# Weight-stationary blocks: three 256-column products into one set of PSUM columns, read in place, with PSUM dealt out anew

## Chip, cores and metric

One core of one Trainium2 chip. The metric is device time of one execution in microseconds. The core's engines that matter here are TensorE (PE for its matmuls, PEld for its weight loads), VectorE (DVE), ScalarE (ACT) and the DMA queue that SyncE (SP) issues. GpSimd does next to nothing.

## What is computed

Two layers of a decoder trunk on one sequence of 256 positions, D_MODEL 2048, all in fp32. Each layer projects the normed residual into many branches, mixes each branch (multi-scale pooling, latent attention "mla", short gated convolution, cross-attention into 256 memory rows), gates it with a SiLU path, projects it back, merges the four with sigmoid gates, and adds an output projection:

```python
h = rms_norm(x, norm_g[l])
proj = h @ w_in[l]
(pv, pz, cq, ckv, kr, mz, cb, cc, cx, cz, xq, xz, gpre) = jnp.split(proj, split_points, axis=-1)
y_pool = pool_mixer(pv, pool_w[l], pool_scale[l]) * silu(pz)
y_mla = mla_mixer(cq, ckv, kr, ...) * silu(mz)
y_conv = conv_mixer(cb, cc, cx, conv_w[l]) * silu(cz)
y_mem = memory_xattn(xq, mem_kv, ...) * silu(xz)
merged = sum(gates[:, :, i] * (y_i @ w_branch[l, i]) for the four branches)
x = x + merged @ w_out[l]
```

## The kernel before

Every large product is taken in split precision. A weight chunk of 128 x 1024 fp32 numbers is loaded (`raw`), ACT rounds it to fp32r (`hi`, line 304), and DVE takes the rest (`lo` = raw - hi, line 305). `raw` has 4 buffers, `hi` and `lo` 3 each. Activations are kept the same way in `op` tiles: for two 128-row halves, 256 columns of hi and then 256 columns of lo. A product is then hi*hi + hi*lo + lo*hi, added up in PSUM.

There are two kinds of blocks. In `tm_block` (lines 317 to 319) the activation is the stationary operand and 512 (288 or 384 in a few) columns of weights move: three matmuls for each piece of the sum. In `fm_block` the weight is stationary and the 256 positions move, which gives the result with channels on partitions. That is used for the branches mz, xz, pv, pz, cc, cx, cb and cz (four blocks of 256 channels each) and, through `fm_tile` alone, for the small `pool_w` products. One `fm_block` is 32 calls of `fm_tile` (two halves of 128 channels, 16 pieces of the sum); both layers have 64 such blocks and 8 small ones of 4 calls, 2080 calls in all. Each call is two matmuls:

```python
T.matmul(ps[:, j, :], hi[:, k, n0 : n0 + P], o[:, half].rearrange("p a s -> p (a s)"), start=first, stop=False)
T.matmul(ps[:, j, :S], lo[:, k, n0 : n0 + P], o[:, half, 0, :], start=False, stop=last)
```

The first multiplies weight hi with hi and lo of the activation side by side (512 columns of PSUM); the second adds weight lo times hi to the first 256. So a result sits in two sets of PSUM columns, and `fm_sum` adds them: ACT copies the second set to SBUF (`fmt`, line 337), DVE adds the first set to it (line 338).

PSUM has eight banks of 512 fp32 columns. The pool `acc` holds three tiles of two banks, which `tm_block` and `fm_block` take in turn; `ms` holds two tiles of one bank for transposes and attention. A block can start only when the readers of the tile whose place it takes are done.

The order of the work on each engine is made by a scheduler from the program order; weight loads and their `hi` and `lo` are put some way ahead. In the mla stage a written sequence of steps (`SEQUENCE`) mixes short `tm_block`s ("uq", "ukv"), attention steps and eight `fm_block`s (mz and xz). In the pool stage come four pv blocks, then twice: two pz blocks with SiLU (`silu_half`), and two small products with `pool_w`. The conv stage has sixteen blocks in a row.

Of the kernel before, what the change touches and what calls it, by code (L numbers as in the profile page):

```python
# [10 lines left out]
F32 = mybir.dt.float32  # L11
F32R = mybir.dt.float32r
I32 = mybir.dt.int32
AF = mybir.ActivationFunctionType
ALU = mybir.AluOpType
AX = mybir.AxisListType

P = 128
# [6 lines left out]
S = 256  # L25
# [85 lines left out]
def tile_hybrid_trunk(  # L111
# [3 lines left out]
    V, A, T = nc.vector, nc.scalar, nc.tensor  # L115
# [4 lines left out]
    op = ctx.enter_context(tc.tile_pool(name="op", bufs=16))  # L120
    tp = ctx.enter_context(tc.tile_pool(name="tp", bufs=7))
    sp = ctx.enter_context(tc.tile_pool(name="sp", bufs=4))
    accp = ctx.enter_context(tc.tile_pool(name="accp", bufs=3, space=bass.MemoryType.PSUM))
    msp = ctx.enter_context(tc.tile_pool(name="msp", bufs=2, space=bass.MemoryType.PSUM))

    uid = [0]
# [1 line left out]
    def nm(s):  # L128
        uid[0] += 1
        return f"{s}{uid[0]}"  # L130

    def t4(s):
        return tp.tile([P, 1152], F32, tag="t4", name=nm(s))

    def acc():
        return accp.tile([P, 2, 512], F32, tag="acc", name=nm("acc"))

    def ms():
        return msp.tile([P, 512], F32, tag="ms", name=nm("ms"))
# [4 lines left out]
    def t2(s):  # L144
        return tp.tile([P, 512], F32, tag="t2", name=nm(s), bufs=7)

    def opnd():
        return op.tile([P, 2, 2, S], F32R, tag="op", name=nm("op"))
# [29 lines left out]
    def gcol(vec, name, i):  # L178
        c = VEC_ROWS[name][0] + i
        return vec["gt"][:, c : c + 1]  # L180
# [112 lines left out]
    def wchunks(l, name, c0):  # L293
        off, n, nk, kt = plan[name, c0]
        m = nk * n
        for k0 in range(0, kt, nk):
            raw = wp.tile([P, 1024], F32, tag="raw", name=nm("raw"), bufs=4)
            hi = wp.tile([P, 1024], F32R, tag="hi", name=nm("hi"), bufs=3)
            lo = wp.tile([P, 1024], F32R, tag="lo", name=nm("lo"), bufs=3)
            o = off + P * n * k0  # L300
            step()
            with tc.high_priority(AHEAD):
                nc.sync.dma_start(raw[:, :m], weights[l, o : o + P * m].rearrange("(p m) -> p m", p=P))
                A.copy(hi[:, :m], raw[:, :m])  # L304
                V.tensor_tensor(lo[:, :m], raw[:, :m], hi[:, :m].bitcast(F32), ALU.subtract)  # L305
            yield k0, nk, kt, n, *(w[:, :m].rearrange("p (k n) -> p k n", n=n) for w in (hi, lo))
# [13 lines left out]
        return ps  # L320

    def fm_tile(ps, j, hi, lo, o, half, k, n0, first, last):
        T.matmul(ps[:, j, :], hi[:, k, n0 : n0 + P], o[:, half].rearrange("p a s -> p (a s)"), start=first, stop=False)  # L323
        T.matmul(ps[:, j, :S], lo[:, k, n0 : n0 + P], o[:, half, 0, :], start=False, stop=last)  # L324

    def fm_block(rhs, l, name, c0):
        ps = acc()
        for k0, nk, kt, n, hi, lo in wchunks(l, name, c0):
            for j in range(2):
                for k in range(nk):  # L330
                    kk = k0 + k
                    fm_tile(ps, j, hi, lo, rhs[kk // 2], kk % 2, k, j * P, kk == 0, kk == kt - 1)
        return ps

    def fm_sum(dst, ps):
        tmp = t2("fmt").rearrange("p (n s) -> p n s", n=2)
        A.copy(tmp, ps[:, :, S:])  # L337
        V.tensor_tensor(dst, ps[:, :, :S], tmp, ALU.add)  # L338

    def split(o, src):  # L340
        A.copy(o[:, :, 0, :], src)
        V.tensor_tensor(o[:, :, 1, :], src, o[:, :, 0, :].bitcast(F32), ALU.subtract)
# [145 lines left out]
    def silu_half(z, i, h, l, c0):  # L488
        ps = fm_block(h, l, "in", c0 + 256 * i)
        sl = slice(2 * i, 2 * i + 2)  # L490
        fm_sum(z[:, sl, :], ps)
        sg = t2("sg").rearrange("p (n s) -> p n s", n=2)
        A.activation(sg, z[:, sl, :], AF.Sigmoid)  # L493
        V.tensor_tensor(z[:, sl, :], z[:, sl, :], sg, ALU.mult)  # L494

    def silu_tile():
        return t4("z")[:, :1024].rearrange("p (n s) -> p n s", n=4)
# [1 line left out]
    def silu_block(h, l, c0):  # L499
        z = silu_tile()  # L500
        for i in range(2):
            silu_half(z, i, h, l, c0)
        return z
# [226 lines left out]
    def pool_branch(l, vec, h):  # L730
        mixed = []
        for b in range(2):
            for i in range(2):
                ps = fm_block(h, l, "in", OFF["pv"] + 512 * b + 256 * i)
                g = 2 * b + i
                w = WINDOWS[g]
                v = t4("pv")[:, :544].rearrange("p (n s) -> p n s", n=2)
                nc.gpsimd.memset(v[:, :, :16], 0.0)
                fm_sum(v[:, :, 16:], ps)
                s = v  # L740
                sh = 1
                while sh < w:
                    n = t4("ps")[:, :544].rearrange("p (n s) -> p n s", n=2)
                    a = 2 * sh - 1
                    V.tensor_tensor(n[:, :, a:], s[:, :, a:], s[:, :, a - sh : 272 - sh], ALU.add)
                    s = n
                    sh *= 2
                fix = cst[:, C_FIX + 16 * g : C_FIX + 16 * (g + 1)].unsqueeze(1).broadcast_to([P, 2, 16])
                V.tensor_tensor(s[:, :, 16:32], s[:, :, 16:32], fix, ALU.mult)
                V.scalar_tensor_tensor(s[:, :, 16:], s[:, :, 16:], 1.0 / w, v[:, :, 16:], ALU.mult, ALU.subtract)  # L750
                o = opnd()
                split(o, s[:, :, 16:])
                mixed.append(o)
        ys = []
        for b in range(2):
            sz = silu_block(h, l, OFF["pz"] + 512 * b)
            (_, _, _, _, hi, lo), = wchunks(l, "pool", 512 * b)
            for i in range(2):
                g = 2 * b + i
                ps = acc()  # L760
                for j in range(2):
                    for k in range(2):
                        fm_tile(ps, j, hi, lo, mixed[g], k, 2 * i + k, j * P, k == 0, k == 1)
                y = t2("yp").rearrange("p (n s) -> p n s", n=2)
                fm_sum(y, ps)
                for j in range(2):
                    V.scalar_tensor_tensor(
                        y[:, j, :], y[:, j, :], gcol(vec, "pool_scale", 2 * g + j), sz[:, 2 * i + j, :], ALU.mult, ALU.mult
                    )
                o = opnd()  # L770
                split(o, y)
                ys.append(o)
        return ys

    def conv_branch(l, vec, h):
        ys = []
        for b in range(2):
            cc = t4("cc")[:, :1024].rearrange("p (n s) -> p n s", n=4)
            for i in range(2):
                ps = fm_block(h, l, "in", OFF["cc"] + 512 * b + 256 * i)  # L780
                fm_sum(cc[:, 2 * i : 2 * i + 2, :], ps)
            u = t4("u")[:, :1032].rearrange("p (n s) -> p n s", n=4)
            nc.gpsimd.memset(u[:, :, :2], 0.0)
            for i in range(2):
                ps = fm_block(h, l, "in", OFF["cx"] + 512 * b + 256 * i)
                sl = slice(2 * i, 2 * i + 2)
                fm_sum(u[:, sl, 2:], ps)
                V.tensor_tensor(u[:, sl, 2:], u[:, sl, 2:], cc[:, sl, :], ALU.mult)
            y = cc
            for n in range(4):  # L790
                w = [gcol(vec, "conv_w", 8 * j + 4 * b + n) for j in range(3)]
                V.tensor_scalar(y[:, n, :], u[:, n, 0:S], w[0], None, ALU.mult)
                V.scalar_tensor_tensor(y[:, n, :], u[:, n, 1 : S + 1], w[1], y[:, n, :], ALU.mult, ALU.add)
                V.scalar_tensor_tensor(y[:, n, :], u[:, n, 2 : S + 2], w[2], y[:, n, :], ALU.mult, ALU.add)
            bb = t4("cb")[:, :1024].rearrange("p (n s) -> p n s", n=4)
            for i in range(2):
                ps = fm_block(h, l, "in", OFF["cb"] + 512 * b + 256 * i)
                sl = slice(2 * i, 2 * i + 2)
                fm_sum(bb[:, sl, :], ps)
                V.tensor_tensor(y[:, sl, :], y[:, sl, :], bb[:, sl, :], ALU.mult)  # L800
            sz = silu_block(h, l, OFF["cz"] + 512 * b)
            ys += gated_out([y], [sz])
        return ys
# [58 lines left out]
    for l in range(DEPTH):  # L862
# [4 lines left out]
        vec = vecs[l]  # L867
# [28 lines left out]
        def filler(_):  # L896
            dst, name, b, i = fill.pop(0)
            if i == 0:
                dst[b] = silu_tile()
            silu_half(dst[b], i, h, l, OFF[name] + 512 * b)  # L900
# [7 lines left out]
        o, sz = xq, sxz  # L908
# [75 lines left out]
```

## Time and profile before

| | |
|---|---|
| median of 3 runs | 2520.2 us (2517.4 to 2521.82) |
| span of the profiled execution | 2517.2 us, so 3.0 us less than the median of the runs |
| PE busy | 2503.9 us, 99% of the span |
| DVE busy, ACT busy | 1539.0 us (61%), 1248.4 us (50%) |
| DMA | 484 MB, mean 192 GB/s |
| TensorE clock granted | full speed in all 40 slices |

Which of the three runs the profile belongs to is not recorded. The time of a PE matmul in the profile runs from its start to a modelled end, and neighbours overlap; what a matmul costs a dense stream is the distance from its start to the next one's start. A timeline row gives the start in microseconds, then the duration, engine, line, operation, the tiles, the shape and a count.

### The profile page before, as it was taken

The numbers are of one execution on the slowest core, as the hardware profiler recorded it, in microseconds if no ns is written. First come the engines' busy times: TensorE is split into PE (matmuls) and PEld (weight loads), VectorE is DVE, ScalarE is ACT, GpSimd is POOL, SyncE is SP. The second block draws the span as 40 slices with busy tenths as digits, with TensorE's granted clock in tenths as the row PEclk, the third lists the DMA queues.
The fourth block names the chain that finished last, engine by engine and source line by source line (L and its number), as shares of the span: only waits on it lengthen the run. The fifth ranks groups of instructions, "written<-read, shape, count | busy, mean of one in ns | idle before, by whom it ended". The sixth has DMA issues, their size and how long they took to land.

```text
span 2517.2 us, 32451 instructions
## 1 busy us (share of the span) xinstructions
PE 2503.9 (99%) x12402; PEld 2108.3 (84%) x12402; DVE 1539.0 (61%) x2132; ACT 1248.4 (50%) x1707; POOL 1.6 (0%) x16
## 2 busy tenths in 40 slices
PE   8999999999999999999999999999999999999999
PEld 7888888888888888888888888888888888888887
DVE  6767775566556655556474577755765565555554
ACT  7556674445444444445454566744444444444443
POOL 0000000000000000000000000000000000000000
PEclk9999999999999999999999999999999999999999
DMA  8665436655655566667655654366556655566565
GB/s 314 207 198 162 145 128 197 202 188 192 201 196 186 188 221 203 201 195 231 220 187 167 202 166 136 128 202 204 186 191 202 194 187 188 193 202 203 189 229 164
DMA packets 143676, 484.22 MB, mean 192 GB/s; under 512 B 16160, under 2 KB 17184, under 8 KB 143520
## 3 DMA queue, kind: packets, MB, share of 16 engines
q1 hardware_dynamic: 142800, 481.06, 58.5%
q8 instruction: 97, 1.59, 0.3%
q10 hardware_dynamic: 720, 1.09, 0.1%
q14 instruction: 59, 0.48, 0.1%
HBM read 477.89 MB, written 4.19 MB: 192 GB/s over the span
## 4 chain that ended last, share of the span: by engine, by line
PE 97%; DVE 1%; ACT 1%; DMA 0%; issue 0%; DVEq 0%; SPq 0%; ACTq 0%
PE acc L319 22%; PE acc L318 22%; PE acc L317 22%; PE acc L323 19%; PE acc L324 10%; PE ms L703 1%; PE ms L702 1%; PE ms L350 1%; DVE lo L305 0%; ACT junk L197 0%; PE ms L551 0%; PE ms L552 0%; PE ms L553 0%; DMA row<-in_x_dram 0%; ACT hi L304 0%; PE ms L722 0%
## 5 line engine op out<-in xcount | busy, mean ns | idle before, releaser
L305 DVE TENSOR_TENSOR lo<-raw,hi 128x1024 fp32r<-128x1024 f32 (+2 forms) x884 | 1062.4, 1202 | 869.8 <-ACT hi L304 867.0
L304 ACT CAST hi<-raw 128x1024 fp32r<-128x1024 f32 (+2 forms) x884 | 914.7, 1035 | 1179.1 <-PE acc L319 791.2
L317 PE MATMUL acc<-hi,op 128*128 128x512 f32 (+2 forms) x2496 | 962.5, 386 | 5.8 <-ACT op L392 5.7
L318 PE MATMUL acc<-lo,op 128*128 128x512 f32 (+2 forms) x2496 | 957.9, 384 | 1.7 <-DVE lo L305 1.7
L319 PE MATMUL acc<-hi,op 128*128 128x512 f32 (+2 forms) x2496 | 958.1, 384 | 0.0
L323 PE MATMUL acc<-op,hi 128*128 128x512 f32 x2080 | 736.9, 398 | 0.1
L324 PE MATMUL acc<-op,lo 128*128 128x256 f32 x2080 | 585.7, 282 | 0.0
L317 PEld LDWEIGHTS acc<-hi,op 128*128 128x128 f32 x2496 | 469.2, 188 | 95.2 <-ACT op L392 6.2
L319 PEld LDWEIGHTS acc<-hi,op 128*128 128x128 f32 x2496 | 469.0, 188 | 92.0 <-issue 1.3
L318 PEld LDWEIGHTS acc<-lo,op 128*128 128x128 f32 x2496 | 469.4, 188 | 91.1 <-DVE lo L305 2.9
L323 PEld LDWEIGHTS acc<-op,hi 128*128 128x128 f32 x2080 | 390.8, 188 | 94.3 <-DVE z L338 0.8
L324 PEld LDWEIGHTS acc<-op,lo 128*128 128x128 f32 x2080 | 392.9, 189 | 1.9 <-issue 1.3
L814 DVE TENSOR_TENSOR g<-acc,gb 128x1024 f32<-128x1024 f32 x32 | 39.2, 1224 | 12.7 <-PE acc L319 12.7
L337 ACT COPY fmt<-acc 128x512 f32<-128x512 f32 x72 | 41.4, 581 | 0.0
L815 ACT ACTIVATE g<-g 128x1024 f32<-128x1024 f32 x32 | 34.0, 1062 | 6.7 <-DVE g L814 6.7
L821 DVE TENSOR_TENSOR g<-g,acc 128x1024 f32<-128x1024 f32 x24 | 29.3, 1221 | 9.8 <-PE acc L319 9.8
L822 DVE TENSOR_TENSOR merged<-merged,g 128x1024 f32<-128x1024 f32 x24 | 29.2, 1219 | 0.0
L513 ACT ACTIVATE sm<-sm,smx,rqs 128x128 f32<-128x128 f32 (+1 forms) x32 | 17.3, 540 | 22.3 <-DVE smx L511 22.3
L494 DVE TENSOR_TENSOR z<-z,sg 128x512 f32<-128x512 f32 x32 | 22.0, 688 | 7.8 <-ACT sg L493 7.7
L197 ACT ACTIVATE junk<-acc 128x256 f32<-128x256 f32 (+2 forms) x68 | 25.2, 371 | 2.1 <-PE acc L319 1.2
L392 ACT ACTIVATE op<-ms,gt 128x256 fp32r<-128x256 f32 x32 | 15.1, 471 | 14.0 <-DVE op L393 14.0
L338 DVE TENSOR_TENSOR z<-acc,fmt 128x512 f32<-128x512 f32 x32 | 21.9, 684 | 0.0
(193 smaller groups left out, 949.1 us busy)
## 6 DMA issues: line engine op xcount, KB each, us to landing
raw<-in_weights_dram SPq DMA_DIRECT2D x836, 512.0 KB, 3.5
raw<-in_weights_dram SPq DMA_DIRECT2D x32, 288.0 KB, 2.8
gb<-in_gate_b_dram SPq DMA_DIRECT2D x32, 256.0 KB, 4.4
raw<-in_weights_dram SPq DMA_DIRECT2D x16, 384.0 KB, 3.1
mt<-in_memT_dram SPq DMA_DIRECT2D x14, 256.0 KB, 5.7
row<-in_mem_dram SPq DMA_DIRECT2D x4, 512.0 KB, 8.4
row<-in_x_dram SPq DMA_DIRECT2D x4, 512.0 KB, 8.2
xt<-in_xT_dram SPq DMA_DIRECT2D x8, 256.0 KB, 5.5
```

The source lines that it names most:

```text
L304: A.copy(hi[:, :m], raw[:, :m])
L305: V.tensor_tensor(lo[:, :m], raw[:, :m], hi[:, :m].bitcast(F32), ALU.subtract)
L317: T.matmul(ps[:, t, :n], hh, hi[:, k, :], start=kk == 0, stop=False)
L318: T.matmul(ps[:, t, :n], hh, lo[:, k, :], start=False, stop=False)
L319: T.matmul(ps[:, t, :n], hl, hi[:, k, :], start=False, stop=kk == kt - 1)
L323: T.matmul(ps[:, j, :], hi[:, k, n0 : n0 + P], o[:, half].rearrange("p a s -> p (a s)"), start=first, stop=False)
L324: T.matmul(ps[:, j, :S], lo[:, k, n0 : n0 + P], o[:, half, 0, :], start=False, stop=last)
L337: A.copy(tmp, ps[:, :, S:])
L814: V.tensor_tensor(g, pg, gb.unsqueeze(1).broadcast_to([P, 2, 512]), ALU.add)
L815: A.activation(g, g, AF.Sigmoid)
L821: V.tensor_tensor(g, g, pb, ALU.mult)
L822: V.tensor_tensor(mg, mg, g, ALU.add)
```

## The change

`fm_tile` now issues three matmuls of 256 columns, all into the same 256 PSUM columns: weight hi times activation hi, weight hi times activation lo, weight lo times activation hi. Both 128-channel halves of a block fit one bank, in a new tile `fm` (two buffers in the pool of `ms`); the bank is cleared once, by the first matmul of the first half. `acc` goes from three tiles to two and is left to `tm_block`. PSUM is full before (3 x 2 + 2 banks) and after (2 x 2 + 2 + 2). The sum on DVE is gone: `silu_half`, the pool products and the conv stage read the PSUM tile where they need it, twice in `silu_half` (the sigmoid on ACT, the product on DVE); pv and cc are copied out by ACT. The number of 128-row columns that TensorE streams is the same (512 + 256 = 3 x 256); the matmuls grow by 2080.

```diff
--- before.py
+++ after.py
@@ -120,7 +120,7 @@
     op = ctx.enter_context(tc.tile_pool(name="op", bufs=16))
     tp = ctx.enter_context(tc.tile_pool(name="tp", bufs=7))
     sp = ctx.enter_context(tc.tile_pool(name="sp", bufs=4))
-    accp = ctx.enter_context(tc.tile_pool(name="accp", bufs=3, space=bass.MemoryType.PSUM))
+    accp = ctx.enter_context(tc.tile_pool(name="accp", bufs=2, space=bass.MemoryType.PSUM))
     msp = ctx.enter_context(tc.tile_pool(name="msp", bufs=2, space=bass.MemoryType.PSUM))
 
     uid = [0]
@@ -134,6 +134,9 @@
 
     def acc():
         return accp.tile([P, 2, 512], F32, tag="acc", name=nm("acc"))
+
+    def fms():
+        return msp.tile([P, 2, S], F32, tag="fm", name=nm("fm"))
 
     def ms():
         return msp.tile([P, 512], F32, tag="ms", name=nm("ms"))
@@ -320,11 +323,13 @@
         return ps
 
     def fm_tile(ps, j, hi, lo, o, half, k, n0, first, last):
-        T.matmul(ps[:, j, :], hi[:, k, n0 : n0 + P], o[:, half].rearrange("p a s -> p (a s)"), start=first, stop=False)
-        T.matmul(ps[:, j, :S], lo[:, k, n0 : n0 + P], o[:, half, 0, :], start=False, stop=last)
+        wh, wl = hi[:, k, n0 : n0 + P], lo[:, k, n0 : n0 + P]
+        T.matmul(ps[:, j, :], wh, o[:, half, 0, :], start=first and j == 0, stop=False, skip_group_check=True)
+        T.matmul(ps[:, j, :], wh, o[:, half, 1, :], start=False, stop=False, skip_group_check=True)
+        T.matmul(ps[:, j, :], wl, o[:, half, 0, :], start=False, stop=last, skip_group_check=True)
 
     def fm_block(rhs, l, name, c0):
-        ps = acc()
+        ps = fms()
         for k0, nk, kt, n, hi, lo in wchunks(l, name, c0):
             for j in range(2):
                 for k in range(nk):
@@ -333,9 +338,7 @@
         return ps
 
     def fm_sum(dst, ps):
-        tmp = t2("fmt").rearrange("p (n s) -> p n s", n=2)
-        A.copy(tmp, ps[:, :, S:])
-        V.tensor_tensor(dst, ps[:, :, :S], tmp, ALU.add)
+        A.copy(dst, ps)
 
     def split(o, src):
         A.copy(o[:, :, 0, :], src)
@@ -488,10 +491,9 @@
     def silu_half(z, i, h, l, c0):
         ps = fm_block(h, l, "in", c0 + 256 * i)
         sl = slice(2 * i, 2 * i + 2)
-        fm_sum(z[:, sl, :], ps)
         sg = t2("sg").rearrange("p (n s) -> p n s", n=2)
-        A.activation(sg, z[:, sl, :], AF.Sigmoid)
-        V.tensor_tensor(z[:, sl, :], z[:, sl, :], sg, ALU.mult)
+        A.activation(sg, ps, AF.Sigmoid)
+        V.tensor_tensor(z[:, sl, :], ps, sg, ALU.mult)
 
     def silu_tile():
         return t4("z")[:, :1024].rearrange("p (n s) -> p n s", n=4)
@@ -757,15 +759,14 @@
             (_, _, _, _, hi, lo), = wchunks(l, "pool", 512 * b)
             for i in range(2):
                 g = 2 * b + i
-                ps = acc()
+                ps = fms()
                 for j in range(2):
                     for k in range(2):
                         fm_tile(ps, j, hi, lo, mixed[g], k, 2 * i + k, j * P, k == 0, k == 1)
                 y = t2("yp").rearrange("p (n s) -> p n s", n=2)
-                fm_sum(y, ps)
                 for j in range(2):
                     V.scalar_tensor_tensor(
-                        y[:, j, :], y[:, j, :], gcol(vec, "pool_scale", 2 * g + j), sz[:, 2 * i + j, :], ALU.mult, ALU.mult
+                        y[:, j, :], ps[:, j, :], gcol(vec, "pool_scale", 2 * g + j), sz[:, 2 * i + j, :], ALU.mult, ALU.mult
                     )
                 o = opnd()
                 split(o, y)
@@ -784,20 +785,17 @@
             for i in range(2):
                 ps = fm_block(h, l, "in", OFF["cx"] + 512 * b + 256 * i)
                 sl = slice(2 * i, 2 * i + 2)
-                fm_sum(u[:, sl, 2:], ps)
-                V.tensor_tensor(u[:, sl, 2:], u[:, sl, 2:], cc[:, sl, :], ALU.mult)
+                V.tensor_tensor(u[:, sl, 2:], ps, cc[:, sl, :], ALU.mult)
             y = cc
             for n in range(4):
                 w = [gcol(vec, "conv_w", 8 * j + 4 * b + n) for j in range(3)]
                 V.tensor_scalar(y[:, n, :], u[:, n, 0:S], w[0], None, ALU.mult)
                 V.scalar_tensor_tensor(y[:, n, :], u[:, n, 1 : S + 1], w[1], y[:, n, :], ALU.mult, ALU.add)
                 V.scalar_tensor_tensor(y[:, n, :], u[:, n, 2 : S + 2], w[2], y[:, n, :], ALU.mult, ALU.add)
-            bb = t4("cb")[:, :1024].rearrange("p (n s) -> p n s", n=4)
             for i in range(2):
                 ps = fm_block(h, l, "in", OFF["cb"] + 512 * b + 256 * i)
                 sl = slice(2 * i, 2 * i + 2)
-                fm_sum(bb[:, sl, :], ps)
-                V.tensor_tensor(y[:, sl, :], y[:, sl, :], bb[:, sl, :], ALU.mult)
+                V.tensor_tensor(y[:, sl, :], y[:, sl, :], ps, ALU.mult)
             sz = silu_block(h, l, OFF["cz"] + 512 * b)
             ys += gated_out([y], [sz])
         return ys
```

The scheduler moves little else. Three places bear on the prediction. The first is DVE in the pool stage of the first layer, around the end of the second pz block and the two small products; there, `z` is the SiLU tile, `yp` the pool result, `lo` a weight chunk, `gt` the small vectors. Before:

```order
L305 TENSOR_TENSOR lo_5339<-raw_5337,hi_5338 128x1024
L305 TENSOR_TENSOR lo_5361<-raw_5359,hi_5360 128x1024
L338 TENSOR_TENSOR z_5102<-acc_5198,fmt_5287 128x512
L305 TENSOR_TENSOR lo_5383<-raw_5381,hi_5382 128x1024
L494 TENSOR_TENSOR z_5102<-z_5102,sg_5290 128x512
L338 TENSOR_TENSOR yp_5308<-acc_5299,fmt_5309 128x512
L338 TENSOR_TENSOR yp_5326<-acc_5317,fmt_5327 128x512
L767 SCALAR_TENSOR_TENSOR yp_5308<-yp_5308,gt_83,z_5102 128x256
```

Now, on the same engine at the same place:

```order
L308 TENSOR_TENSOR lo_5751<-raw_5749,hi_5750 128x1024
L308 TENSOR_TENSOR lo_5781<-raw_5779,hi_5780 128x1024
L496 TENSOR_TENSOR z_5454<-fm_5579,sg_5700 128x512
L768 SCALAR_TENSOR_TENSOR yp_5722<-fm_5709,gt_83,z_5454 128x256 x2
L345 TENSOR_TENSOR op_5725<-yp_5722,op_5725 128x2x256
L768 SCALAR_TENSOR_TENSOR yp_5741<-fm_5728,gt_83,z_5454 128x256
```

The second pz block is `acc_5198` before and `fm_5579` now. Its last reader was the sum of line 338, behind `lo_5361`; now it is the product of line 496, behind `lo_5781`, the same two chunks further on. The two small products were `acc_5299` and `acc_5317` and are `fm_5709` and `fm_5728`.

The second place is PE at the same point: the last call of `fm_tile` of the first small product and the first of the second. Now:

```order
L327 MATMUL fm_5709<-op_5046,hi_5704 128x256
L328 MATMUL fm_5709<-op_5046,hi_5704 128x256
L329 MATMUL fm_5709<-op_5046,lo_5705 128x256
L327 MATMUL fm_5728<-op_5179,hi_5704 128x256
L328 MATMUL fm_5728<-op_5179,hi_5704 128x256
```

With two `fm` tiles in turn, `fm_5728` takes the place of `fm_5579`; before, the third `acc` tile stood between, and it was the next pz block that took the place of `acc_5198`.

The third place is PE in the mla stage, where the block "uq" of the first head pair (`acc_1943`) ends and its "ukv" (`acc_1994`) begins. Before:

```order
L318 MATMUL acc_1943<-lo_1964,op_1358 128x384
L319 MATMUL acc_1943<-hi_1963,op_1358 128x384
L317 MATMUL acc_1994<-hi_1996,op_1678 128x512
L318 MATMUL acc_1994<-lo_1997,op_1678 128x512
L319 MATMUL acc_1994<-hi_1996,op_1678 128x512
```

Now:

```order
L321 MATMUL acc_1943<-lo_1964,op_1358 128x384
L322 MATMUL acc_1943<-hi_1963,op_1358 128x384
L530 MATMUL ms_2079<-cst,qr_1913 128x128 x4
L530 MATMUL ms_2104<-cst,qr_1913 128x128
L320 MATMUL acc_1994<-hi_1996,op_1678 128x512
```

Five transposes of `qr` that stood behind `acc_1994` now stand in front of it. `acc_1994` now takes the place of the second "xq" block (`acc_1754`), two `tm_block`s back.

## Prediction

> **What bounds the kernel now.** I read the page's busy times first, then the chain that ended last, then the waits of PE.
>
> ```profile
> span 2517.2 us, 32451 instructions
> PE 2503.9 (99%) x12402; PEld 2108.3 (84%) x12402; DVE 1539.0 (61%) x2132; ACT 1248.4 (50%) x1707; POOL 1.6 (0%) x16
> PEclk9999999999999999999999999999999999999999
> PE 97%; DVE 1%; ACT 1%; DMA 0%; issue 0%; DVEq 0%; SPq 0%; ACTq 0%
> PE acc L319 22%; PE acc L318 22%; PE acc L317 22%; PE acc L323 19%; PE acc L324 10%; PE ms L703 1%; PE ms L702 1%; PE ms L350 1%; DVE lo L305 0%; ACT junk L197 0%; PE ms L551 0%; PE ms L552 0%; PE ms L553 0%; DMA row<-in_x_dram 0%; ACT hi L304 0%; PE ms L722 0%
> L323 PE MATMUL acc<-op,hi 128*128 128x512 f32 x2080 | 736.9, 398 | 0.1
> L324 PE MATMUL acc<-op,lo 128*128 128x256 f32 x2080 | 585.7, 282 | 0.0
> L337 ACT COPY fmt<-acc 128x512 f32<-128x512 f32 x72 | 41.4, 581 | 0.0
> L338 DVE TENSOR_TENSOR z<-acc,fmt 128x512 f32<-128x512 f32 x32 | 21.9, 684 | 0.0
> L814 DVE TENSOR_TENSOR g<-acc,gb 128x1024 f32<-128x1024 f32 x32 | 39.2, 1224 | 12.7 <-PE acc L319 12.7
> ```
>
> ```profile
> PE acc L317 <- ACT op L392: 5.7, 1, 5.7
> PE acc L318 <- DVE lo L305: 1.7, 1, 1.7
> PE ms L680 <- DVE yf L725: 0.5, 2, 0.2
> ```
>
> PE is the bound: 97% of the chain, at the full clock throughout. All that the view of waits shows of PE standing idle is 7.9 us, nearly all of it for work of the start (lines 392 and 305). So the 72 copies and 72 sums that vanish (41.4 us of ACT, some 49 us of DVE at 0.684) buy nothing directly: no PE time waits on them. What counts is how fast PE streams the 2080 tiles of lines 323 and 324, 29% of the chain, and whether new waits for PSUM appear.
>
> **The pace of the stream.** The durations of matmul rows overlap, so I take start to start. First and last rows of long stretches, from timelines of PE:
>
> ```profile
> 859.99 0.40 PE L323 MATMUL acc<-op,hi 128*128 128x512 f32 x1
> 876.59 0.40 PE L323 MATMUL acc<-op,hi 128*128 128x512 f32 x1
> ...
> 228.16 0.39 PE L323 MATMUL acc<-op,hi 128*128 128x512 f32 x1
> 231.97 0.39 PE L323 MATMUL acc<-op,hi 128*128 128x512 f32 x1
> ...
> 340.22 0.28 PE L552 MATMUL ms<-op,op 128*128 128x256 f32 x1
> 340.33 0.28 PE L553 MATMUL ms<-op,op 128*128 128x256 f32 x1
> 340.45 0.28 PE L551 MATMUL ms<-op,op 128*128 128x256 f32 x1
> ...
> 342.85 0.28 PE L324 MATMUL acc<-op,lo 128*128 128x256 f32 x1
> ...
> 929.83 0.39 PE L317 MATMUL acc<-hi,op 128*128 128x512 f32 x1
> 940.71 0.39 PE L317 MATMUL acc<-hi,op 128*128 128x512 f32 x1
> ...
> 122.46 0.30 PE L317 MATMUL acc<-hi,op 128*128 128x288 f32 x1
> 123.92 0.30 PE L319 MATMUL acc<-hi,op 128*128 128x288 f32 x1
> ```
>
> - Today's tile, 512 + 256 columns: 47 tiles in 16.60 us in the conv stage, 353 ns each. A count over the stage agrees:
>
> ```profile
> 727.00:895.00 168.00, 168.00 (x477) 89.40 (x476) 1.00 0.56 187
> ```
>
>   That is line 323 alone: 168.00 us over 476 loads is 353 ns. In parts of the mla stage the same tile takes 346 ns (11 tiles in 3.81 us). Why there are two paces the profile does not tell.
> - 512 columns alone (`tm_block`): 48 matmuls in 10.88 us, 227 ns.
> - 288 columns alone: 11 in 1.46 us, 133 ns. From these two, (227 - 133) / 224 = 0.42 ns a column and some 12 ns for each matmul whatever its size; 256 columns should then take 119 to 120 ns.
> - 256 columns alone, in cross-attention: 21 matmuls from 340.33 to 342.85, 2.52 us, 120 ns; the first two gaps are shorter, 0.23 us together. This is the nearest row: lines 551 to 553 are hi*hi, hi*lo, lo*hi of 256 columns, each with its own weight load, three in a row into one set of PSUM columns, which is what the new `fm_tile` does.
>
> **The change part by part.**
>
> 1. Three matmuls for two. Columns are equal, the fixed part is paid once more. A new tile is 3 x 120 = 360 ns against 353: +7 ns, 2080 x 6.7 = +13.9 us. Of the 512 tiles of the mla stage I count half as running at 346 ns today; for those 256 it is 7 ns more, +1.8 us. The ends: 115 ns, the first two gaps of that stretch, would give 345 and -16 us; 133 ns, the longest sustained row, would give 399 and +97 us. I take 120, since that row has size, loads and target of the new work; the short gaps do not last, and 133 belongs to 288 columns and holds only if a short burst flatters the 120.
>
> The Trainium skill, "TensorE: Matmul & The Clock Gate", section Back-to-back issue gap, gives N / 2.4 + 2.5 ns for a warm matmul. By it the tile would go from 216 + 109 = 325 to 3 x 109 = 328 ns, an estimate of +5 us over all tiles; the trace has 227 where it says 216 and 120 where it says 109, so the fixed part here is some 12 ns and not 2.5, and the measurement decides.
>
> 2. The second weight load of the same weights. `tm_block` already issues two matmuls in a row with one stationary operand (lines 317 and 318) and loads it twice; the page counts as many loads as matmuls (12402 each). I cost the extra 2080 loads at nothing beyond the 120 ns, since the 120 rows carry one load each. If the stream did not cover them, the 133 ns of the 288-column rows would be the nearest upper bound (the +97 us of step 1).
>
> 3. Two `fm` tiles where three `acc` tiles served: the pool stage. The timelines of PE, DVE and ACT around the end of the second pz block:
>
> ```profile
> 567.36 0.40 PE L323 MATMUL acc<-op,hi 128*128 128x512 f32 x1
> ...
> 568.77 0.40 PE L323 MATMUL acc<-op,hi 128*128 128x512 f32 x1
> ...
> 570.06 0.28 PE L324 MATMUL acc<-op,lo 128*128 128x256 f32 x1
> 570.40 0.49 PE L323 MATMUL acc<-op,hi 128*128 128x512 f32 x1
> ```
>
> ```profile
> 567.44 1.05 ACT L304 CAST hi<-raw 128x1024 fp32r<-128x1024 f32 x1 [1.73 <-PE acc L323]
> ...
> 568.52 1.23 DVE L305 TENSOR_TENSOR lo<-raw,hi 128x1024 fp32r<-128x1024 f32 x1 [1.55 <-ACT hi L304]
> 569.66 0.68 DVE L338 TENSOR_TENSOR z<-acc,fmt 128x512 f32<-128x512 f32 x1
> ```
>
> ```profile
>   PEld acc L317: 0.8, 2
>   PEld acc L323: 0.8, 2
> ```
>
> The pz block ends at 567.36. Its chunk frees a weight buffer, ACT and DVE convert the next chunk first, and the last reader of the pz tile ends only at 569.66 + 0.68 = 570.34. The next pz block, third in the ring, starts at 570.40, 0.06 later, though the stream was due at 570.18: a wait of 0.22 us, one of four that line 338 causes (last fence). In the new order the product of line 496 stands behind the same conversion, so it ends near 570.35 (0.69 long). But now the second small product needs that place, and the first is done at 567.36 + 4 x 0.36 = 568.80. PE waits 570.41 - 568.80 = 1.6 us, less the 0.22 of today: +1.4 us, four times, +5.6 us. Behind it nothing is late: the next pz block needs line 768 on the first small product, two instructions of 0.48 (today's line 767), done at 571.3, and PE gets there at 571.85. If the reader were served before the conversion, the wait would shrink to about nothing; if one more conversion slips ahead, it grows by 1.2 each.
>
> ```profile
> L767 DVE SCALAR_TENSOR_TENSOR yp<-yp,gt,z 128x256 f32<-128x256 f32 x16 | 7.0, 478 | 0.0
> ```
>
> 4. Two `acc` tiles for `tm_block`. The tight place is "ukv" of the first pair:
>
> ```profile
> 198.06 0.39 PE L317 MATMUL acc<-hi,op 128*128 128x512 f32 x1
> ...
> 198.60 0.19 ACT L197 ACTIVATION_READ_ACCUMULATOR junk<-acc 128x1 f32 x1
> ...
> 225.39 0.60 PE L680 MATMUL ms<-cst,qg 128*128 128x128 f32 x4
> 225.83 0.60 PE L685 MATMUL ms<-cst,kn 128*128 128x128 f32 x4
> ```
>
> It started at 198.06 and would now have to wait for the last sum of squares of "xq", 198.79. Five transposes moved in front fill 5 x 0.11 = 0.55 us of that; some 0.2 us is left, in each layer: +0.4 us. In the gate stage DVE reads a block as soon as it is done and needs 1.2 us (line 814), and the block behind it takes eight or sixteen pieces of six matmuls of 227 ns, 11 us or more; nothing waits there.
>
> 5. Removed work on ACT and DVE: cost nothing, gain nothing, since PE covers them; if PE were to speed up, DVE at 61% would still have room.
>
> Sum: 13.9 + 1.8 + 5.6 + 0.4 = +21.7 us, from a span of 2517.2 to 2538.9; with the 3.0 us between span and median, 2542 us.
>
> **Rivals.**
>
> A. The 256s do not hold 120 ns in a long stream. For it: the 120 is seen over some 23 matmuls only, and today's mixed tile runs at 353 though 227 + 120 makes 347, so a slip of 6 to 7 ns a tile exists. Against it: 512s and 288s alone hold their pace. With the same slip, 367 ns, a further 14 us on the forecast: 2556 us. It decides from 121 ns a matmul up.
>
> The same page of the Trainium skill, section Wait — 56ns, not 53.3ns?, says that a matmul decoded by firmware costs 62 ns of the sequencer; were a load to cost as much, a pair would take 124 ns and a tile 372, an estimate of 2567 us. The transposes above pass at 110 ns a pair, in short bursts that a queue may have held ready, so the trace speaks against it without excluding it.
>
> B. The 256s run at 117 ns, between the short gaps and the 120. The tile takes 351 ns, 3 us less in all than today's tiles, and the 6 us of waits take that and 3 more: 2523 us, no change that can be told. For it: the two short gaps at the start of the stretch. Against: the 21 rows at 120 behind them.
>
> C. Faster: two matmuls in a row on one stationary operand stream like one of 512, so the tile is 227 + 120 = 347 ns throughout. That takes some 14 us off the tiles that run at 353; less 6 us of waits, -8 us, 2512 us. It is faster than before from 350 ns a tile down, by more than can be told apart from 347.5 down. Against it: lines 317 and 318 share their operand, and their gap is that of lines 318 and 319, 48 at 227 with none shorter.
>
> D. The two `acc` tiles and the moved attention steps cost more: PE waits of 1 to 2 us at some of the eight mla steps, 2548 us. Against it: only one place of the ring is tight.
>
> **Chances.** Forecast 0.62, A 0.17, B 0.11, C 0.07, D 0.03. What this kernel's measurement can tell from no change is about 0.2%, 5 us. C is faster, B the same but for a tenth of it that ends over the bound, the others slower: faster 0.07, same 0.10, slower 0.83. The range goes down to B and up to A: 2521 to 2557; the likeliest case alone is 2535 to 2548.
>
> **What would show it.** Right: line 327 to 327 in the conv stage 360 ns; PE waits of 1.6 us at four places of the pool stage, put down to DVE z L496; ACT and DVE busy less by some 40 to 90 us with PE still at 99%. Wrong: 351 or 367 ns a tile; no waits in the pool stage; or waits of line 320 on ACT and DVE beyond half a microsecond a layer.

## The result and the profile after

The changed kernel takes 2540.6 us (median of 4 runs, 2539.0 to 2543.4) where the one before takes 2520.7 (4 runs): a ratio of 1.0085, 95% interval 1.0072 to 1.0098. It is slower by 20 us; 2542 was forecast. The profiled execution took 2539.9 us and its span is 2538.1.

The page of the changed kernel, its busy times, the chain and the groups of the new tile:

```profile
span 2538.1 us, 36485 instructions
PE 2521.5 (99%) x14482; PEld 2221.1 (88%) x14482; DVE 1498.2 (59%) x2060; ACT 1220.8 (48%) x1651; POOL 1.6 (0%) x16
PE 97%; DVE 1%; ACT 1%; DMA 1%; issue 0%; SPq 0%; DVEq 0%; ACTq 0%
L327 PE MATMUL fm<-op,hi 128*128 128x256 f32 x2080 | 591.4, 284 | 3.1 <-DVE z L496 3.1
L329 PE MATMUL fm<-op,lo 128*128 128x256 f32 x2080 | 589.9, 284 | 0.0
L328 PE MATMUL fm<-op,hi 128*128 128x256 f32 x2080 | 589.8, 284 | 0.0
```

DVE lost 41 us of work and ACT 28, PE is as full as before, and the span grew by 20.9. The three groups show 284 ns a matmul, as line 324 had 282, but these durations run to modelled ends that overlap and say nothing of the pace. The pace is in the starts. The first line of the new tile in the conv stage, first row and 50 tiles on, and a count over the stage (that line alone, matmuls and then loads):

```profile
733.72 0.28 PE L327 MATMUL fm<-op,hi 128*128 128x256 f32 x1
...
751.72 0.28 PE L327 MATMUL fm<-op,hi 128*128 128x256 f32 x1
```

```profile
735.00:915.00 180.00, 141.74 (x501) 96.10 (x500) 1.00 0.56 184
```

50 tiles in 18.00 us and 500 loads in 180.00 us: 360 ns a tile, three times 120, where the tile before took 353. What PE waited for:

```profile
PE acc L320 <- ACT op L395: 5.7, 1, 5.7
PE fm L327 <- DVE z L496: 3.1, 2, 1.5
PE acc L321 <- DVE lo L308: 1.7, 1, 1.7
PE acc L322 <- DVE op L396: 0.3, 1, 0.3
PE ms L692 <- DVE mw L688: 0.3, 1, 0.3
```

The waits of the start are those of before (5.7 and 1.7). New, but for two of 0.3 us, are two waits on the product of line 496, 1.5 us each. Timelines of DVE and PE at the first of them, in the pool stage of the first layer:

```profile
573.57 1.22 DVE L308 TENSOR_TENSOR lo<-raw,hi 128x1024 fp32r<-128x1024 f32 x1 [1.66 <-ACT hi L307]
574.71 0.68 DVE L496 TENSOR_TENSOR z<-fm,sg 128x512 f32<-128x512 f32 x1
```

```profile
573.73 0.28 PE L329 MATMUL fm<-op,lo 128*128 128x256 f32 x1
575.54 0.36 PE L327 MATMUL fm<-op,hi 128*128 128x256 f32 x1 [1.53 <-DVE z L496]
```

The reader of the second pz block ends at 574.71 + 0.68 = 575.39, behind the conversion of a chunk, and PE begins the second small product at 575.54. From the last matmul's start it is 1.81 us in place of 0.12, a loss of 1.69. At the second such place of the layer there is no wait. PE there:

```profile
601.40 0.28 PE L329 MATMUL fm<-op,lo 128*128 128x256 f32 x1
601.52 0.40 PE L320 MATMUL acc<-hi,op 128*128 128x512 f32 x1
...
602.91 0.39 PE L320 MATMUL acc<-hi,op 128*128 128x512 f32 x1
603.22 0.36 PE L327 MATMUL fm<-op,hi 128*128 128x256 f32 x1
```

Between the two small products stand seven matmuls of the gate block that follows (line 320 at 601.52 to line 320 at 602.91, 0.23 each). They belong to the other pool of PSUM tiles, need nothing that is late, and fill the time.

By stage, from the first matmul of the weight-stationary blocks in it to the first of what follows, with the second layer in brackets: the mla stage took 151.0 us (151.1) and takes 154.5 (154.2); the pool stage 96.2 (96.6), now 101.4 (101.4), of which 1.6 are the seven gate matmuls that moved in, and the stretch behind it is shorter by 1.7; the conv stage 180.9, now 184.3, in both layers. Ahead of the first mla stage nothing changed; the stretches behind the two mla stages and the one ahead of the second are longer by 0.3 us each. These differences add up to the 20.9 us of the span. The conv stage has 512 tiles and no waits: 3.42 us / 512 = 6.7 ns a tile.

### The profile page after: what moved, and what is told of

The parts are those of the page before. It is cut to its first block, busy times and chain, and to the rows that moved or that the text cites. A ratio compares the mean times of both kernels' runs of the same rounds, so it can differ in the third digit from the quotient of the medians.

```text
span 2538.1 us, 36485 instructions
## 1 busy us (share of the span) xinstructions
PE 2521.5 (99%) x14482; PEld 2221.1 (88%) x14482; DVE 1498.2 (59%) x2060; ACT 1220.8 (48%) x1651; POOL 1.6 (0%) x16
## 4 chain that ended last, share of the span: by engine, by line
PE 97%; DVE 1%; ACT 1%; DMA 1%; issue 0%; SPq 0%; DVEq 0%; ACTq 0%
PE acc L322 21%; PE acc L320 21%; PE acc L321 21%; PE fm L327 10%; PE fm L328 10%; PE fm L329 10%; PE ms L705 1%; PE ms L704 1%; PE ms L353 1%; DVE lo L308 0%; PE ms L724 0%; ACT hi L307 0%; PE ms L553 0%; DMA row<-in_x_dram 0%; PE ms L554 0%; PE ms L555 0%
## 5 line engine op out<-in xcount | busy, mean ns | idle before, releaser
L327 PE MATMUL fm<-op,hi 128*128 128x256 f32 x2080 | 591.4, 284 | 3.1 <-DVE z L496 3.1
L329 PE MATMUL fm<-op,lo 128*128 128x256 f32 x2080 | 589.9, 284 | 0.0
L328 PE MATMUL fm<-op,hi 128*128 128x256 f32 x2080 | 589.8, 284 | 0.0
L327 PEld LDWEIGHTS fm<-op,hi 128*128 128x128 f32 x2080 | 399.4, 192 | 5.1 <-issue 4.7
L329 PEld LDWEIGHTS fm<-op,lo 128*128 128x128 f32 x2080 | 399.5, 192 | 0.7 <-issue 0.7
L328 PEld LDWEIGHTS fm<-op,hi 128*128 128x128 f32 x2080 | 399.5, 192 | 0.4
L496 DVE TENSOR_TENSOR z<-fm,sg 128x512 f32<-128x512 f32 x32 | 22.0, 687 | 6.2 <-ACT sg L495 6.2
```

Of the source, the lines that this page charges most:

```text
L327: T.matmul(ps[:, j, :], wh, o[:, half, 0, :], start=first and j == 0, stop=False, skip_group_check=True)
L328: T.matmul(ps[:, j, :], wh, o[:, half, 1, :], start=False, stop=False, skip_group_check=True)
L329: T.matmul(ps[:, j, :], wl, o[:, half, 0, :], start=False, stop=last, skip_group_check=True)
```

## The experiments

### The split alone

The kernel before, with its 512-column matmul cut in two. PSUM tiles, `fm_sum` and all readers stay.

```diff
-        T.matmul(ps[:, j, :], hi[:, k, n0 : n0 + P], o[:, half].rearrange("p a s -> p (a s)"), start=first, stop=False)
+        T.matmul(ps[:, j, :S], hi[:, k, n0 : n0 + P], o[:, half, 0, :], start=first, stop=False, skip_group_check=True)
+        T.matmul(ps[:, j, S:], hi[:, k, n0 : n0 + P], o[:, half, 1, :], start=False, stop=last, skip_group_check=True)
```

> The kernel before, with its 512-column matmul split into two of 256 (weight hi times activation hi, weight hi times activation lo); PSUM tiles, the sum on ACT and DVE and all readers stay as before. Theory (each matmul pays some 12 to 13 ns whatever its size, and that is most of the change): a tile takes 360 ns for 353, line to same line, the conv stage gets 3.4 us longer, the whole 14 to 17 us longer (2535 to 2538), with the small waits of the pool stage as before. Rival (the added time of the changed kernel lies in the new PSUM rings and their waits): within 4 us of before. Rival (three matmuls into the same 256 columns are what costs): 351 or less a tile here, no change.

Measured: 2535.6 us against 2519.2, ratio 1.0062 (1.0047 to 1.0077): +16.3 us. A count of its line 323 in the conv stage, and its waits of PE:

```profile
735.00:915.00 180.00, 141.50 (x501) 96.00 (x500) 1.00 0.56 184
```

```profile
PE acc L317 <- ACT op L393: 5.7, 1, 5.7
PE acc L318 <- DVE lo L305: 1.7, 1, 1.7
```

360 ns a tile here too, though the second product goes to other PSUM columns, and the conv stage is 184.3 us as in the changed kernel. So the one set of columns costs nothing and saves nothing on PE; the third matmul is some 16 of the 20 us. The rival that puts it all on the PSUM rings is out, and so is a cost of adding into the same columns.

### The small pool products in other banks

```diff
-                ps = fms()
+                ps = ms().rearrange("p (j s) -> p j s", j=2)
```

This stands in `pool_branch` of the changed kernel alone.

> The changed kernel, with the eight small pool products in tiles of the transposes' tag (two other banks) in place of the fm tag. Theory (two waits of 1.7 us in the pool stage come from the ring of two fm tiles): both waits of line 327 on DVE z disappear, 3 us less than the changed kernel, 2537 to 2538. Rival (the conversion ahead of the reader holds PE in another way): a wait of the same size appears at the next pz block.

Measured: 2538.4 us, ratio 1.0071 (1.0056 to 1.0086); span 2536.4, 1.7 less than that of the changed kernel. Its waits of PE:

```profile
PE acc L320 <- ACT op L395: 5.7, 1, 5.7
PE acc L321 <- DVE lo L308: 1.8, 1, 1.8
PE acc L320 <- ACT hi L307: 0.6, 1, 0.6
PE ms L692 <- DVE mw L688: 0.3, 1, 0.3
```

Both waits on line 496 are gone and none of their size came at the next pz block: the ring of two `fm` tiles made them. The pool stage and the stretch behind it together are 1.9 us shorter in each layer. The span fell by 1.7 us only, because the work ahead of the first mla stage, which the edit does not touch, took 2.2 us longer in this execution (216.3 for 214.1 us; in that of the split alone it took 216.0). The gain in the whole is less than the 3 us expected, and its size lies within the spread of the runs; what is shown is that the waits go, and 3.9 us of these stages with them.

### The second and third matmul exchanged

```diff
-        T.matmul(ps[:, j, :], wh, o[:, half, 1, :], start=False, stop=False, skip_group_check=True)
-        T.matmul(ps[:, j, :], wl, o[:, half, 0, :], start=False, stop=last, skip_group_check=True)
+        T.matmul(ps[:, j, :], wl, o[:, half, 0, :], start=False, stop=False, skip_group_check=True)
+        T.matmul(ps[:, j, :], wh, o[:, half, 1, :], start=False, stop=last, skip_group_check=True)
```

> The changed kernel, with the second and third matmul of a tile exchanged (hi*hi, lo*hi, hi*lo), so that no two neighbours of a tile share the stationary operand. Theory (each matmul loads its weights and pays the same whether or not the neighbour had them): 360 ns a tile, within 3 us of the changed kernel. Rival (a load of the weights that are already there is cheaper, or dearer): the tile changes by some 5 to 12 ns, the time by 10 to 25 us.

Measured: 2539.1 us, ratio 1.0078 (1.0061 to 1.0095). The count of line 327 in the conv stage is that of the split alone, row for row:

```profile
735.00:915.00 180.00, 141.50 (x501) 96.00 (x500) 1.00 0.56 184
```

A tile takes 360 ns whether or not a neighbour has the same weights. Loading them once more costs nothing beyond the matmul's own pace, and having them already saves nothing: rival C had no ground.

### The sizes grouped, in the kernel before

Today's tile took 353 ns where one matmul of 512 and one of 256 by themselves make 347. Two orders with fewer changes of size, with the same products and PSUM tiles: by two, and by a whole chunk of eight.

```diff
-            for j in range(2):
-                for k in range(nk):
-                    kk = k0 + k
-                    fm_tile(ps, j, hi, lo, rhs[kk // 2], kk % 2, k, j * P, kk == 0, kk == kt - 1)
+            for k in range(nk):
+                kk = k0 + k
+                o, half = rhs[kk // 2], kk % 2
+                for j in range(2):
+                    T.matmul(ps[:, j, :], hi[:, k, j * P : (j + 1) * P], o[:, half].rearrange("p a s -> p (a s)"), start=kk == 0, stop=False)
+                for j in range(2):
+                    T.matmul(ps[:, j, :S], lo[:, k, j * P : (j + 1) * P], o[:, half, 0, :], start=False, stop=kk == kt - 1)
```

In the second version the loop over `k` is closed and opened again ahead of the last two lines.

> The kernel before, with its matmuls in another order: for each piece of the sum two of 512 columns (both 128-channel halves), then two of 256, in place of 512, 256, 512, 256. Same products, same PSUM tiles. Theory that the slow pace of today's tile (353 where 227 + 120 makes 347) is a cost of each change of size: half the changes, 350 ns or a little less, 5 to 12 us faster than before (2508 to 2516). Rival (it belongs to the operands or to the stage, not to the order): 353 stays, no change within 3 us. Rival (512 after 512 with weights from hi and a moving op tile has its own slow pace): slower than before.

> The kernel before, with the matmuls of a whole chunk grouped: eight of 512 columns in a row, then eight of 256. Theory (each matmul costs its columns and a fixed 13 ns, and a change of size costs some 3 ns more): 347 ns a tile, the conv stage 177.7 us, 2508 to 2511 us, a little faster than the grouping by two. Rival (what the grouping by two gained is not the number of changes): 353 again or 348 as there. If 512 after 512 stays at 233 ns with weights stationary where tm_block has 227, the tile comes to 350.

Measured: by two, 2511.2 us, ratio 0.9966 (0.9953 to 0.9979); by a chunk, 2510.4 us, ratio 0.9963 (0.9951 to 0.9976). Timelines of PE in the conv stage, by two and then by a chunk (xN merges N matmuls in a row):

```profile
766.01 0.62 PE L333 MATMUL acc<-op,hi 128*128 128x512 f32 x2
...
770.19 0.62 PE L333 MATMUL acc<-op,hi 128*128 128x512 f32 x2
```

```profile
801.24 2.00 PE L333 MATMUL acc<-op,hi 128*128 128x512 f32 x8
803.08 1.11 PE L338 MATMUL acc<-op,lo 128*128 128x256 f32 x8
804.03 2.00 PE L333 MATMUL acc<-op,hi 128*128 128x512 f32 x8
```

By two: twelve tiles in 4.18 us, 348 ns. By a chunk: eight of 512 in 1.84 us, 230 ns each, eight of 256 in 0.95 us, 119 each, together 349 ns. Both versions beat the kernel before and the changed one, by some 9 and 30 us, with nothing but the order of the matmuls changed. The pace expected of the chunk version (347) is not reached, and it is no better than grouping by two, so a price for each change of size is not the whole account: with a fourth of the changes there should have been more left to gain. What is left is in the 512s, 230 ns where `tm_block` has 227, though seven of eight follow another 512.

That these orders are faster is shown; why is not. The alternation of 512 and 256 does not by itself cost the 6 ns. In the mla stage of the kernel before, the same two lines in the same order run at 346 to 347 ns for 26 tiles on end:

```profile
228.16 0.39 PE L323 MATMUL acc<-op,hi 128*128 128x512 f32 x1
...
237.17 0.39 PE L323 MATMUL acc<-op,hi 128*128 128x512 f32 x1
```

These are 9.01 us. This stretch begins behind four small attention matmuls, in the middle of a block; the conv stage, where nothing comes between, keeps to 353 over all its 512 tiles. What puts a stretch on the one pace or the other was not tested. Nor was a second thing that the new orders change: in them neighbouring matmuls of a size write in turn to the two PSUM banks of a block, where the kernel before stays in one bank for a whole half of the chunk.

### Each matmul in two halves

```diff
-        T.matmul(ps[:, j, :], wh, o[:, half, 0, :], start=first and j == 0, stop=False, skip_group_check=True)
-        ...
+        for w, a, e in ((wh, 0, False), (wh, 1, False), (wl, 0, last)):
+            for c in range(2):
+                cs = slice(c * P, (c + 1) * P)
+                st = first and j == 0 and a == 0 and c == 0 and w is wh
+                T.matmul(ps[:, j, cs], w, o[:, half, a, cs], start=st, stop=e, skip_group_check=True)
```

> The changed kernel, with each 256-column matmul cut into two of 128 columns. Same columns, twice the matmuls. Theory A (a fixed 13 ns a matmul and nothing else): 6 x 66.7 = 400 ns a tile, +83 us, 2624 us. Theory B (under some 108 ns the weight load sets the pace, as the transposes' 108.5 ns suggests): 6 x 108.5 = 651 ns a tile, +605 us, 3145 us. In between: a floor of the sequencer between 67 and 108 ns.

Measured, in a single run: 3231.3 us, span 3229.5. The count in its conv stage (its one matmul line, matmuls and then loads) and a timeline:

```profile
935.00:1235.00 300.00, 300.00 (x2689) 300.00 (x2688) 1.00 0.29 99
```

```profile
999.90 0.61 PE L331 MATMUL fm<-op,hi 128*128 128x128 f32 x4
1000.34 0.39 PE L331 MATMUL fm<-op,lo 128*128 128x128 f32 x2
1000.57 0.61 PE L331 MATMUL fm<-op,hi 128*128 128x128 f32 x4
```

2688 loads in 300.00 us: 112 ns for a matmul of 128 columns, 670 ns a tile, near the 651 of theory B and far from the 400 of a fixed part alone. So in this stream something other than the columns holds a pair of load and matmul to 112 ns, and the 120 ns of 256 columns lies just above that floor. Fewer columns than 128 were not tried. Whether the load itself or the issue of two instructions sets it was not told apart.

## Why the prediction was right, step by step

**What bounds.** Right: PE is at 99% in both, and 41 us less on DVE and 28 us less on ACT show no gain. With the old readers and sums in place the split alone gives 2535.6; the lighter readers of the changed kernel do not make up for its waits. I had let all 72 copies go, 41.4 us of ACT. The 16 of pv and cc stay (line 341, 9 us), which cost nothing here.

**Step 1, the pace.** Right to the nanosecond: 360 ns a tile from the attention row of 120, conv stage +3.42 us against 512 x 6.7 = 3.43. The row that had the size, the loads and the target of the new work held over the 512 tiles of each conv stage, so rival A (a slip in long streams) is out: pairs of 120 ns ran for 184 us on end. Rival B's short gaps did not last. The mla stages gained 3.5 and 3.1 us where step 1 gives 256 x 6.7 + 128 x 7 = 2.6: 0.9 and 0.5 us too little. (The wait of step 4 lies ahead of them.) In the run with the second and third matmul exchanged, also with two `acc` tiles and 360 ns a tile, they gained 2.5 and 2.2 us; there the scheduler mixed the attention matmuls in otherwise. So the excess is neither the pace nor the number of `acc` tiles; it seems to go with that mix, which was not followed further. My count of half the tiles at 346 ns was too high as well: of the 512 tiles, 171 are followed by the next at 345 to 348 ns.

The Trainium skill, "TensorE: Matmul & The Clock Gate", section Back-to-back issue gap, gives N / 2.4 + 2.5 ns for a warm matmul by itself, so the third matmul would cost 2.5 ns, an estimate. The trace does not agree: the split alone measures 6.7 ns against a tile that itself ran 6 ns above its two sizes, and 13 against 347, the sum of the two sizes by themselves.

The same page of the Trainium skill, section Wait — 56ns, not 53.3ns?, gives some 62 ns for a matmul decoded by firmware; if a load cost as much, which the page does not say, a pair would take 124 ns, an estimate. The 120 ns held through a stage show that no such bound is at work here.

**Step 2, the second load.** Right: the exchange shows it. The price of rival C was some 2 us too high: the 1824 tiles taken as running at 353 ns would have gained 6.3 ns each, 11.5 us and not 14.

**Step 3, the pool stage.** This step failed in its count. One wait had the size forecast (1.69 us lost against 1.61), with the reader and the conversion in the order that was read; but "four times" is two. At the second place of each layer the scheduler put seven gate matmuls between the small products. I had followed PE's order at the first place only. Two times 1.69, less the four short waits of before (0.22 to 0.28 each, all gone), is +2.4 us net where I had 5.6. By stages, the pool stages with the stretches behind them gained 6.6 us where steps 1 and 3 give 9.2. The 2.6 us too much there stand against 1.3 too little in the mla stages and 0.5 elsewhere, so that the total, 2540.6 for 2542, is as near as it is partly by luck.

**Step 4.** Right: behind five transposes, "ukv" of the first pair waited little. Timelines of PE and ACT there, first layer:

```profile
197.72 0.71 PE L530 MATMUL ms<-cst,qr 128*128 128x128 f32 x5
198.50 0.50 PE L320 MATMUL acc<-hi,op 128*128 128x512 f32 x1
```

```profile
198.26 0.19 ACT L200 ACTIVATION_READ_ACCUMULATOR junk<-acc 128x1 f32 x1
```

It starts 0.78 us behind the first transpose, of which five at 0.11 fill 0.55; some 0.2 us is left for waiting, as forecast. The last sum of squares of "xq" ends at 198.26 + 0.19 = 198.45, just ahead of it. Of rival D only the 1.3 us of the mla stages shows; PE has no wait of a microsecond there, so two `acc` tiles are enough for `tm_block`.

## What to carry to other kernels

Where TensorE is the bound, count matmuls as well as columns: a saving of work on engines that nobody waits for is worth nothing, and one more matmul a tile, even at equal columns, was paid 2080 times here. Price a new pattern from the row that has its size, its loads and its target, start to start, not from the row's duration. When a ring of buffers gets shorter, look at the order of the waiting engine at every place where it bites; the scheduler may fill one gap and not the other.

## What was not expected of the hardware

The same matmuls in another order are faster: in the conv stage 512 and 256 in turn take 353 ns a pair, two and two 348. Yet the order in turn has two paces of its own, since it holds 346 to 347 ns in parts of the mla stage; what decides between them stays open. And 128 columns, each matmul with its own 128 x 128 fp32r weights, take 112 ns in a long stream where 256 columns take 120, so a matmul of half the columns takes only 8 ns less.
